# A batched matrix product in fp16: the wait for the last stores moves from SyncE to VectorE

## The chip, the cores and the metric

The kernel runs on one core of one Trainium2 chip. A core has TensorE (PE), VectorE (DVE), ScalarE (ACT), GpSimd (POOL) and SyncE (SP), each with its own instruction stream, and 16 DMA engines. The time is device microseconds of one execution; the median over three runs counts.

## The reference

```python
def setup_inputs():
    batch, dim_i, dim_j, dim_k = 32, 256, 512, 384
    return {
        "x": np.random.randn(batch, dim_i, dim_j).astype(np.float32),
        "y": np.random.randn(batch, dim_j, dim_k).astype(np.float32),
    }

def reference(x, y):
    return np.einsum('bij,bjk->bik', x, y).astype(np.float32)
```

For each of 32 batches a 256 x 512 matrix is multiplied by a 512 x 384 matrix. The inputs are 41.94 MB of float32, the output is 12.58 MB.

## The kernel before

The work is cut into N = 8 groups of Q = 4 batches. For each group SP loads x (2 MB) and y (3 MB), each in one DMA, into one of two buffers of each kind. POOL rounds x to fp16 (`round_x`) and y to fp16 (`round_y`). VectorE transposes x in 32 x 32 blocks (`transpose_x`), as 32-bit words that hold two fp16 numbers. TensorE multiplies: the four batches of a group lie in the four 32-row strips of the array, and a group is done in NE = 2 halves, each of which fills four PSUM banks. ScalarE and VectorE together copy the finished banks from PSUM into the output buffer `o_sb`, which holds the whole output; VectorE has the last five of sixteen blocks of each half (`OWN = 5`).

The order of the work is written out by hand: each engine has its own program with semaphores between them, most of them counted up through the whole kernel. At the head of the kernel stand the first four loads and a barrier of all engines (seen in the profile at lines 265 and 78). There is no barrier of the kernel's own at its end.

SP's program comes next. It loads groups 2 to 7 as buffers come free (lines 69 and 73, which wait on `s_cast`), and then issues three stores (line 96): groups 0 to 4 in one, groups 5 and 6 in one, and group 7. Each adds 16 to the semaphore `s_out` when it is complete. The last store waits for the last copies of ScalarE and VectorE (`s_act`, `s_dve`). Then, at line 110, SP gives a signal (`s_sp`) on which POOL clears all semaphores but `s_out`; and at line 111 SP waits until `s_out` has the 48 of the three stores and takes them off again, so that the next execution starts from zero. This wait is SP's last instruction.

VectorE's program ends in these lines, the last of which copies its share of the last half and signals `s_dve`:

```python
    vector_half(N - 1, 0)
    v.wait_ge(s_pe, chunk_done(N - 1, 1, NC - 1))
    collect(v.tensor_copy, N - 1, 1, BLOCKS[-OWN:], None, s_dve)
```

The copies of both engines are made by the helper `collect`, at line 165, and TensorE's products by `product`, at line 217.

## Time and profile before

| what | value |
|---|---|
| median of three runs | 132.0 us (131.89 to 132.18) |
| the profiled execution's own time | 132.13 us |
| its span, from the first to the last of the kernel's own instructions | 130.8 us |
| busy: PE, DVE, ACT, POOL | 61.4, 82.7, 84.1, 74.2 us |
| moved by DMA: read, written | 41.94 MB, 12.58 MB |
| mean over the span | 417 GB/s |

The profile is one execution. Its times are microseconds from the start of the span unless marked ns. The page gives for each engine a row of 40 digits, the busy tenths of 40 equal slices; further views list the timeline, the waits, the DMA issues, the busy time by windows, and all instructions of a source line. Instructions that only wait or signal (EVENT_SEMAPHORE, DRAIN) are not counted as busy; an engine's own queue of them is marked with a q, as in SPq. A wait is told as "who <- what released it: total us, times, longest".

### The profile page before, as it was taken

Reading aid. Unit: us, or ns where it says so; the run is one execution under the profiler, and the core shown is the slowest. Engines: PE = TensorE matmul, PEld = TensorE weight load, DVE = VectorE, ACT = ScalarE, POOL = GpSimd, SP = SyncE. Lnnn points to the kernel's source line nnn. Section 1 sums busy time; section 2 is a strip of 40 time slices with the busy share of each in tenths; the row PEclk is TensorE's granted clock in tenths of the full one; section 3 lists DMA queues with packets and bytes.
Section 4 is the critical chain, followed back from the end, with each engine's and each line's share of the span. In section 5 each row is a group of like instructions: output and inputs, shape, how many; then the busy total and the mean of one; then the engine's idle time right before and its main releaser. Section 6 shows DMA issues by size and latency. Waiting matters only on the chain. (4 is left out here: it accounts for less than half of the span.)

```text
span 130.8 us, 3199 instructions
## 1 busy us (share of the span) xinstructions
PE 61.4 (47%) x1024; PEld 46.7 (36%) x1024; DVE 82.7 (63%) x144; ACT 84.1 (64%) x178; POOL 74.2 (57%) x42
## 2 busy tenths in 40 slices
PE   0000009910992589089329905980975499100000
PEld 0000009800991566046129604970953236000000
DVE  0000036899379999985997997599999957920000
ACT  0400000599659989993998899399999957994000
POOL 0006991199929965992899459758973970000000
PEclk9999999995589689977986985599599959965555
DMA  5999999999999999999999999999999999999995
GB/s 120 451 396 441 421 431 451 443 408 428 451 413 421 438 443 401 436 436 443 423 458 398 443 408 466 398 418 436 463 398 408 427 438 425 436 428 421 425 440 248
DMA packets 3379, 54.55 MB, mean 417 GB/s; under 512 B 304, under 2 KB 304, under 8 KB 304
## 3 DMA queue, kind: packets, MB, share of 16 engines
q1 hardware_dynamic: 3376, 54.53, 98.1%
q14 instruction: 3, 0.02, 0.0%
HBM read 41.94 MB, written 12.58 MB: 417 GB/s over the span
## 5 line engine op out<-in xcount | busy, mean ns | idle before, releaser
L165 ACT COPY o_sb<-o_ps (+1 forms) x176 | 82.6, 469 | 31.7 <-PE o_ps L217 29.6
L217 PE MATMUL o_ps<-y_r,xt_sb 32*128 32x384 f16 x1024 | 61.4, 384 | 50.4 <-PEq L214 49.5
L217 PEld LDWEIGHTS o_ps<-y_r,xt_sb 32*128 32x128 f16 x1024 | 46.7, 107 | 64.6 <-issue 56.8
L156 DVE STREAM_TRANSPOSE xt_sb<-x_r 128x256 f32<-128x256 f32 x64 | 38.1, 626 | 30.9 <-POOL x_r L126 18.4
L136 POOL CAST y_r<-y_sb 128x1536 f16<-128x1536 f32 (+1 forms) x22 | 44.3, 2049 | 15.8 <-DMA y_sb<-in_y_dram 15.3
L165 DVE COPY o_sb<-o_ps 32x384 f32 (+1 forms) x80 | 44.6, 557 | 1.6
L126 POOL CAST x_r<-x_sb 128x2048 f16<-128x2048 f32 x16 | 30.2, 1893 | 16.8 <-DVE o_sb L165 12.1
L202 ACT ACT_TABLE_LOAD x1 | 1.3, 1283 | 3.4 <-PEq L78 3.4
L265 POOL MEMSET const-float32-0.0<- 128x1 f32 x1 | 0.1, 98 | 0.2 <-issue 0.2
L202 ACT COPY spare<-const-float32-0.0 1x1 f32<-1x1 f32 x1 | 0.2, 190 | 0.0
L265 POOL MEMSET const-bfloat16-1.0<- 128x1 bf16 x1 | 0.1, 101 | 0.0
L265 POOL MEMSET const-uint8-127<- 128x1 uint8 x1 | 0.1, 101 | 0.0
L265 POOL MEMSET const-float32-1.0<- 128x1 f32 x1 | 0.1, 98 | 0.0
## 6 DMA issues: line engine op xcount, KB each, us to landing
y_sb<-in_y_dram SPq DMA_DIRECT2D x8, 3072.0 KB, 16.8
x_sb<-in_x_dram SPq DMA_DIRECT2D x8, 2048.0 KB, 17.0
out_dram<-o_sb SPq DMA_DIRECT2D x1, 7680.0 KB, 33.9
out_dram<-o_sb SPq DMA_DIRECT2D x1, 3072.0 KB, 17.3
out_dram<-o_sb SPq DMA_DIRECT2D x1, 1536.0 KB, 11.5
```

The costliest lines, as they stand in the source:

```text
L126: po.tensor_copy(x_r[:, e], x_sb[n % 2][:, e * H : (e + 1) * H]).then_inc(s_cast, 1)
L136: ins = po.tensor_copy(y_r[:, s], y_sb[n % 2][:, s])
L156: v.transpose(xt_w[:, w], words[:, e, w]).then_inc(s_xt, 1)
L165: ins = copy(o_sb[g * PQ : (g + 1) * PQ, n, e, h], o_ps[h * PQ : (h + 1) * PQ, e * Q + g, :K],)
L202: a_.copy(spare, nc.const_aps.tensor(0.0, [1, 1], F32))
L217: return te.add_instruction(mybir.InstMatmult(name=nc.get_next_instruction_name(), start_tensor_calc=start, stop_tensor_calc=stop, tile_si ...
L265: nc = _bacc.Bacc("TRN2", target_bir_lowering=False, num_devices=1)
```

## The change

The wait for the 48 completions of the stores, with the subtraction that sets `s_out` back, is taken from the end of SP's program and stands at the end of VectorE's. It has the same condition and the same effect. In the changed kernel SP's last instruction is the signal to POOL at line 110, and the wait is at line 191; all lines of the kernel between the two places are one lower than before.

```diff
@@ -108,7 +108,6 @@
     sp.wait_ge(s_dve, NE)
     store(N - 1, N)
     sp.sem_inc(s_sp, 1)
-    sp.wait_op(s_out, 16 * 3, "sem-ge").then_inc(s_out, -16 * 3)
 
 
 
@@ -189,6 +188,7 @@
     vector_half(N - 1, 0)
     v.wait_ge(s_pe, chunk_done(N - 1, 1, NC - 1))
     collect(v.tensor_copy, N - 1, 1, BLOCKS[-OWN:], None, s_dve)
+    v.wait_op(s_out, 16 * 3, "sem-ge").then_inc(s_out, -16 * 3)
 
     a_ = nc.scalar
 
```

## The prediction

> **What bounds the kernel now.** I read the page first, for its head, the DMA rows and the chain.

> ```profile
> span 130.8 us, 3199 instructions
> ...
> DMA  5999999999999999999999999999999999999995
> GB/s 120 451 396 441 421 431 451 443 408 428 451 413 421 438 443 401 436 436 443 423 458 398 443 408 466 398 418 436 463 398 408 427 438 425 436 428 421 425 440 248
> ...
> q1 hardware_dynamic: 3376, 54.53, 98.1%
> ...
> ACT 8%; PE 2%; issue 0%
> ```

> All slices of the DMA row but the first and the last stand at 9: one queue keeps the 16 DMA engines busy for 98.1% of the span, at some 430 GB/s. The kernel is bound by its transfers from end to end. The chain of the page must be read with care here: it has 8% ACT and 2% PE because it follows instructions, and stops at the last copy that an instruction made; what runs after that is a store.

> Next the last stretch, in a view by windows (microseconds; busy time and count for PE, weight loads, DVE, ACT, POOL; then granted clock, DMA share, GB/s):

> ```profile
> core 0: us, PE busy (x) PEld busy (x) DVE busy (x) ACT busy (x) POOL busy (x), PEclk, DMA share, GB/s
> 109.80:119.30 9.50, 1.94 (x46) 1.19 (x37) 5.21 (x10) 9.21 (x20) 0.00 (x0) 0.78 1.00 427
> 119.30:130.30 11.00, 0.00 (x0) 0.00 (x0) 0.00 (x0) 0.00 (x0) 0.00 (x0) 0.50 0.93 398
> 130.30:130.80 0.50, 0.00 (x0) 0.00 (x0) 0.00 (x0) 0.00 (x0) 0.00 (x0) 0.50 0.00 0
> ```

> From 119.3 no engine computes, and the DMA engines work on alone to about 130.3. In the last half microsecond nothing moves any more: the completions of the last store are on their way. The changed instruction waits for just these. The timeline, the DMA issues and the waits of SP's queue give its place:

> ```profile
> 109.44 5.73 DVE L165 COPY o_sb<-o_ps 32x384 f32<-32x384 f32 x10
> ...
> 118.78 0.47 ACT L165 COPY o_sb<-o_ps 32x384 f32<-32x384 f32 x1
> 119.27 0.34 SPq L96 DMA_DIRECT2D out_dram<-o_sb  x1
> ```

> ```profile
> out_dram<-o_sb SPq DMA_DIRECT2D x1, 1536.0 KB, 11.5
> ```

> ```profile
> SPq L96 <- PE o_ps L217: 24.9, 2, 23.5
> SPq L111 <- SPq L111: 11.1, 1, 11.1
> SPq L108 <- DVE o_sb L165: 5.0, 1, 5.0
> SPq L96 <- ACT o_sb L165: 4.0, 1, 4.0
> ```

> The last store is issued at 119.27 and lands 11.5 us later: 119.27 + 11.5 = 130.77. SP's wait at L111, the longest of the tail with 11.1 us, ends there, and with it the span of 130.8. The profiled execution took 132.13 us, so 132.13 - 130.8 = 1.33 us lie around the span, before the first or behind the last of the kernel's own instructions; the trace does not divide them. The profiled time stands 0.1% above the median of 132.0.

> **The change, part by part.** Three things happen.

> SP loses one instruction. Its row, and the rows that show what the same kind of instruction costs on SP and on DVE (duration in ns: least, median, most; then first and last start in us), from the barriers at the head of the kernel:

> ```profile
> L111 SPq EVENT_SEMAPHORE  x1: 17/17/17, 130.8 to 130.8; - x1
> ```

> ```profile
> L78 POOLq EVENT_SEMAPHORE  x4: 17/17/17, 2.9 to 3.3; - x4
> L78 SPq DRAIN  x3: 7/7/123, 2.7 to 3.1; - x3
> ...
> L78 DVEq DRAIN  x2: 10/10/10, 0.8 to 3.2; - x2
> ...
> L78 SPq EVENT_SEMAPHORE  x2: 17/17/17, 3.0 to 3.4; - x2
> ...
> L78 DVEq EVENT_SEMAPHORE  x2: 21/21/21, 3.0 to 3.4; - x2
> ```

> The instruction takes 17 ns on SP and an instruction of its kind 21 ns on DVE. Both are released by the same landing at 130.77. So the end of the span moves by 21 - 17 = +4 ns. In both barrier rounds of L78 the two engines' waits start together at the tenth of a microsecond that the row shows (3.0 and 3.4), so a later wake-up of DVE is under 0.1 us; the term for the span is +0.00 to +0.10 us, and I take +0.00, since the rows are equal at that resolution.

> DVE gets that instruction behind its last copy. Is anything queued behind it? Nothing: it is the last of DVE's program, and DVE's ten last copies end at 109.44 + 5.73 = 115.17. The signal that SP needs from DVE for the last store is given by the last of these copies, ahead of the new wait. The wait that it starts at 115.17 lasts till 130.77, 15.6 us, and delays nobody. Cost zero; the cover is not needed, as no engine waits for DVE after that copy. No queue or DMA moves: the three stores are issued by the same instructions, at the same places, on SP. POOL's clearing of semaphores hangs on the signal that SP gives behind the last store, ahead of L111, and so stands as it is.

> What is left is the 1.33 us around the span. SP now reaches the end of its program at 119.27 + 0.34 = 119.61, plus 17 ns for the signal to POOL, some 11 us before the end, and DVE is the engine that is last. Whatever an engine does between its last instruction and the end of the execution was done by SP behind the landing; now SP does its share under the store, and DVE does its own behind the landing. The trace of before shows no row of that. Bounds: if all 1.33 us were SP's own work, and hid, the gain would be 1.33 us; if all of it were work of the engine that is last, and ran on DVE in the ratio of the rows above, the loss would be between 1.33 x (21/17 - 1) = 0.31 us and 1.33 x (10/7 - 1) = 0.57 us. The nearest row to such work is a barrier round of L78: SP's two waits start at 3.0 and 3.4, so a round of all engines costs some 0.4 us, of which SP and DVE have a drain and a wait each, 7 + 17 = 24 ns against 10 + 21 = 31 ns. A round with DVE last instead of SP thus differs by 7 ns. By that row I take 0.00 us for the exchange.

> [...] Row: 17 ns on SP, 21 ns on DVE, a ratio of 1.24. [...]

> Sum against the profiled execution: 132.13 + 0.00 (SP's instruction against DVE's) + 0.00 (DVE's queue) + 0.00 (what is around the span) = 132.13 us; against the median 132.0 us. I forecast 132.0 us. A difference of under 0.2%, 0.26 us, is about what a measurement of this kernel can tell from none.

> **The rivals.**

> Slower: DVE is the slower one to finish. Mechanism: behind the landing come further instructions of the runtime on the engine that is last, and each takes 21/17 to 10/7 of SP's time. For it speaks the ratio in two kinds of instruction; against it, that only a part of the 1.33 us can lie on that engine, as the rest is ahead of the first instruction or on others. Price at its full size +0.31 to +0.57 us, the middle +0.4 us: 132.4 us. It decides from the point at which about 0.86 us of the 1.33 are such work (0.26 / 0.31 x 1.33 = 1.1 us by the smaller ratio, 0.26 / 0.57 x 1.33 = 0.61 us by the larger, mean 0.86).

> Faster: SP has work of its own at its end, for which the others wait, and it now lies under the last store. For it speaks that SP is the engine that issued every transfer, and that its longest drain in L78, with transfers just issued, took 123 ns where DVE's took 10 ns; and there are 11 us of cover. Against it: two of SP's three drains there took 7 ns, less than DVE's. Price: one round like those of L78, 0.4 us, gone from the path: 131.6 us. It would need 0.26 us, two drains of 123 ns, to be seen. The extreme, with all 1.33 us gone, is 130.7 us, and no row makes it likely.

> That the change does not do what it says can hardly be: the wait needs all 48 counts of the three stores, wherever it stands. A variant is that DVE's wait ends late, because DVE has been idle for 15.6 us. The nearest rows are the waits of L78, after a pause of some 2 us: under 0.1 us later than SP. That stays within the forecast.

> **How the numbers follow.** The forecast, no difference beyond 0.2%, gets 0.42: every term that a row carries is of nanoseconds, but the part that would decide is the one that the trace does not show. Faster, 131.6 us: 0.30. Slower, 132.4 us: 0.28; the bound on it is firmer, since two ratios support it, but it needs most of the 1.33 us. The likeliest case alone covers 132.0 +- 0.26 us, 131.74 to 132.26. With the rivals' prices and 0.1 us of scatter about each (the three runs before lie between 131.89 and 132.18) the range is 131.5 to 132.5 us; what it leaves out is a gain that goes far beyond one round, or the larger ratio on all 1.33 us: under 2 in 10.

> **What would show it.** In the trace after, the DMA row and the issues are as before, the last store lands about 11.5 us after an issue at about 119.3, SP's last instruction is the signal at about 119.7, and the waits of SP's queue no longer have the entry of 11.1 us. DVE's last instruction is a wait of 21 ns which ends the span at about 130.8. The difference between the execution's own time and its span tells between the three cases: near 1.3 us, the forecast; near 0.9, the faster rival; near 1.7, the slower one. I would be wrong in the mechanism if the span itself changed by more than 0.3 us with the last landing where it was, or if the stores were issued at another time.

## The result, and the profile after

| | before | after |
|---|---|---|
| median | 132.04 us (131.82 to 132.43, 22 runs) | 132.22 us (132.00 to 132.98, 22 runs) |
| the profiled execution's own time | 132.13 us | 132.25 us |
| its span | 130.8 us | 130.8 us |

The ratio is 1.0017, 95% interval 1.0009 to 1.0024: the changed kernel is slower by 0.22 us (0.12 to 0.32). That is under the 0.2% that the prediction called no difference, and inside its range, but with 22 runs it is clear of zero.

The page of the changed kernel, in the lines that answer to those of before:

```profile
span 130.8 us, 3199 instructions
...
DMA  5999999999999999999999999999999999999996
...
q1 hardware_dynamic: 3376, 54.53, 98.3%
...
ACT 8%; PE 4%; issue 0%
```

Its last stretch by windows, with the same columns as before:

```profile
109.80:119.30 9.50, 2.34 (x57) 1.30 (x48) 5.20 (x10) 9.21 (x20) 0.00 (x0) 0.76 1.01 429
119.30:130.30 11.00, 0.00 (x0) 0.00 (x0) 0.00 (x0) 0.00 (x0) 0.00 (x0) 0.50 0.94 400
130.30:130.80 0.50, 0.00 (x0) 0.00 (x0) 0.00 (x0) 0.00 (x0) 0.00 (x0) 0.50 0.00 0
```

And the timeline's last store, its DMA issue, the waits of SP's queue, and the instructions of line 191, where the wait now stands:

```profile
119.27 0.34 SPq L96 DMA_DIRECT2D out_dram<-o_sb  x1
```

```profile
out_dram<-o_sb SPq DMA_DIRECT2D x1, 1536.0 KB, 11.5
```

```profile
SPq L96 <- PE o_ps L217: 25.2, 2, 23.6
SPq L108 <- DVE o_sb L164: 4.6, 1, 4.6
SPq L96 <- ACT o_sb L164: 4.1, 1, 4.1
```

```profile
L191 DVEq EVENT_SEMAPHORE  x1: 21/21/21, 130.8 to 130.8; - x1
```

Nothing else inside the span has changed: the last store is issued at 119.27 and takes 11.5 us, as before; the entry of 11.1 us is gone from SP's queue; a wait of 21 ns on DVE ends the span. In the trace's records the last completion comes at 130.722 and DVE's wait ends at 130.771, 49 ns later; before it was 130.767 and 130.801 on SP, 34 ns. The later start, 28 ns behind the completion instead of 17, is 27 or 28 ns in all four kernels of this document in which VectorE waits for the stores. So 0.015 us of the loss lie in the span. The rest of it lies outside: 132.25 - 130.771 = 1.479 us where it was 132.13 - 130.801 = 1.329 us.

This difference, an execution's own time less its span, is called **the rest** from here on. It is a far sharper measure than the time. The time moves by some tenths of a microsecond from run to run, and the span with it (130.5 to 131.5 us in the 22 runs of the changed kernel); the rest does not. Its mean over these runs is 1.480 us, with a scatter of 0.025 us, no more than the rounding of the listed spans to 0.1 us brings. For the kernel before it is 1.339 us over the 29 runs beside the first experiments, and 1.338 us over the 25 beside the later ones. So the rest grew by 0.141 us, and 0.141 + 0.015 = 0.156 us is the loss that the traces account for, against 0.18 us between the medians and 0.12 to 0.32 us by the ratio's interval.

### The profile page after: what moved, and what is told of

It is laid out like the page before. It is cut to its first block, busy times and chain, and to the rows that moved or that the text cites. A ratio compares the mean times of both kernels' runs of the same rounds, so it can differ in the third digit from the quotient of the medians.

```text
span 130.8 us, 3199 instructions
## 1 busy us (share of the span) xinstructions
PE 62.6 (48%) x1024; PEld 45.2 (35%) x1024; DVE 82.7 (63%) x144; ACT 84.1 (64%) x178; POOL 74.2 (57%) x42
## 3 DMA queue, kind: packets, MB, share of 16 engines
q1 hardware_dynamic: 3376, 54.53, 98.3%
## 5 line engine op out<-in xcount | busy, mean ns | idle before, releaser
L217 PE MATMUL o_ps<-y_r,xt_sb 32*128 32x384 f16 x1024 | 62.6, 388 | 49.5 <-PEq L214 49.5
L217 PEld LDWEIGHTS o_ps<-y_r,xt_sb 32*128 32x128 f16 x1024 | 45.2, 108 | 66.6 <-issue 56.4
## 6 DMA issues: line engine op xcount, KB each, us to landing
out_dram<-o_sb SPq DMA_DIRECT2D x1, 1536.0 KB, 11.5
```

What stands on the lines that cost most here:

```text
L217: return te.add_instruction(mybir.InstMatmult(name=nc.get_next_instruction_name(), start_tensor_calc=start, stop_tensor_calc=stop, tile_si ...
```

## The experiments

Three theories of the 0.14 us stood at first. By the clock theory, what follows the last instruction runs on the engine that is last, in proportion to its instruction times. By the chain theory, the engines meet one after the other, and the place of the engine that arrives last decides, and nothing else (the last-arriver theory of a later expectation). By the third, each engine has a stretch of its own behind its last instruction, and the execution is over when the last of these is.

**The same wait on the three other engines.** In each, the line is taken from SP and put at the end of another engine's program.

```diff
-    sp.wait_op(s_out, 16 * 3, "sem-ge").then_inc(s_out, -16 * 3)
...
# one of these, as the last instruction of its engine
+    a_.wait_op(s_out, 48, "sem-ge").then_inc(s_out, -48)
+    po.wait_op(s_out, 48, "sem-ge").then_inc(s_out, -48)
+    te.wait_op(s_out, 48, "sem-ge").then_inc(s_out, -48)
```

> ScalarE waits for the 48 completions as its last instruction, instead of SyncE. The measure is the execution's own time less its span (the rest): 1.33 us with SyncE as the last engine, 1.48 us with VectorE. Clock theory: what follows the last instruction runs on the last engine, in proportion to its instruction times; a wait takes 17 ns on ScalarE as on SyncE, so the rest is 1.33 us and the time that of the kernel before (132.0 us). Chain theory: the engines meet at the end one after the other, and the place of the last engine in that order decides; ScalarE then has a rest of its own, other than 1.33 by more than 0.03 us, with the sign given by its place.

> GpSimd waits for the 48 completions, behind its clearing of the semaphores. Clock theory: 17 ns for a wait as on SyncE, rest 1.33 us, time 132.0 us. Chain theory: a rest of its own, between that with ScalarE and that with VectorE if the order of the engines is a simple row of them.

> TensorE waits for the 48 completions. Clock theory by instruction times: a wait takes 51 ns there against 17 on SyncE; VectorE's 21 against 17 made 0.15 us, so the work on the last engine is 0.15 / (21/17 - 1) = 0.64 us on SyncE and 1.9 us on TensorE: the rest grows by 1.28 us to 2.6 us and the time to 133.3 us. Chain theory: the rest differs from 1.33 us by some tenths at most, so 1.1 to 1.6 us, and the time lies between 131.8 and 132.3 us.

The last instructions of the three, by their lines, ScalarE first, then GpSimd, then TensorE:

```profile
L209 ACTq EVENT_SEMAPHORE  x1: 17/17/17, 130.8 to 130.8; - x1
```

```profile
L145 POOLq EVENT_SEMAPHORE  x1: 17/17/17, 130.7 to 130.7; - x1
```

```profile
L250 PEldq EVENT_SEMAPHORE  x1: 51/51/51, 131.5 to 131.5; - x1
```

| engine that waits | its wait, ns | mean rest, us (runs) | above SP | ratio of times to before (95%) |
|---|---|---|---|---|
| SyncE (before) | 17 | 1.339 (29) | - | - |
| VectorE (the change) | 21 | 1.480 (22) | 0.141 | 1.0017 (1.0009 to 1.0024) |
| ScalarE | 17 | 1.506 (10) | 0.167 | 1.0013 (1.0001 to 1.0024) |
| TensorE | 51 | 1.616 (8) | 0.277 | 1.0037 (1.0019 to 1.0054) |
| GpSimd | 17 | 1.889 (10) | 0.550 | 1.0037 (1.0024 to 1.0049) |

The clock theory falls. ScalarE's and GpSimd's waits take the same 17 ns as SP's, yet their rests are 0.17 and 0.55 us longer; TensorE's wait is three times as long, and its rest is 1.62 us, not 2.6. That ScalarE has a rest of its own is what the chain theory expected; TensorE's lies just above the 1.1 to 1.6 us that it gave. SP is the best of the five. GpSimd's rest does not lie between ScalarE's and VectorE's either, as a simple row of engines would have it. The times follow the rests less sharply: ScalarE's and VectorE's can't be told apart by them, and TensorE's span was longer in the profiled execution, 131.5 us, because the last completion came late, at 131.445 (two more of its eight runs have spans of 131.3 and 131.4 us).

**A relay: VectorE ends just ahead of SyncE.**

```diff
-    sp.wait_op(s_out, 16 * 3, "sem-ge").then_inc(s_out, -16 * 3)
+    sp.wait_op(s_out, 49, "sem-ge").then_inc(s_out, -49)
...
     collect(v.tensor_copy, N - 1, 1, BLOCKS[-OWN:], None, s_dve)
+    v.wait_op(s_out, 48, "sem-ge").then_inc(s_out, 1)
```

> VectorE waits for the 48 completions and adds one; SyncE waits for 49 and takes them off, so that SyncE is last and VectorE ends just ahead of it. The span grows by the hand-over, some 0.05 us. If VectorE's own work behind its last instruction is what is longer (clock theory), it still ends last: the time is that of the changed kernel, 132.2 us, and the rest, counted from SyncE's end, 1.43 us. If the engine that arrives last alone decides (chain theory), the rest goes back to 1.33 us and the time is 132.1 us.

The two last instructions, DVE's and SP's:

```profile
L192 DVEq EVENT_SEMAPHORE  x1: 21/21/21, 131.3 to 131.3; - x1
```

```profile
L111 SPq EVENT_SEMAPHORE  x1: 17/17/17, 131.4 to 131.4; - x1
```

In the records DVE's wait ends at 131.355 and SP's at 131.397, 0.042 us later. The mean rest, counted from SP's end, is 1.436 us (10 runs). Counted from DVE's end it is 1.436 + 0.042 = 1.478 us: VectorE's 1.480 again, though SP was the last to arrive. The chain theory falls in that form, the last arriver alone; a chain in which each engine also has some work of its own is not excluded by it. The time is 132.23 us, ratio 1.0020 (1.0007 to 1.0032), as the theory of own stretches has it.

**The same relay from GpSimd**, whose stretch is the longest:

```diff
-    sp.wait_op(s_out, 16 * 3, "sem-ge").then_inc(s_out, -16 * 3)
+    sp.wait_op(s_out, 49, "sem-ge").then_inc(s_out, -49)
...
+    po.wait_op(s_out, 48, "sem-ge").then_inc(s_out, 1)
```

> As the relay with VectorE, but GpSimd waits for the 48 completions and adds one, and SyncE waits for 49 and is last. Own-tail theory (each engine has a stretch of its own behind its last instruction, and the execution ends when the last of these ends): GpSimd's is 1.89 us against SyncE's 1.34, so the rest, counted from SyncE's end some 0.05 us later, is 1.84 us, and the time 132.5 us. Last-arriver theory (only the identity of the engine that ends last decides): rest 1.34 us, time 132.1 us.

The mean rest is 1.855 us (10 runs). GpSimd's wait ends at 130.486 in the records, SP's at 130.528, 0.042 us later; 1.889 - 0.042 = 1.847 us was due. The time is 132.54 us, ratio 1.0037 (1.0024 to 1.0050).

**The relay with a gap.** VectorE hands over as in the first relay, but SP has some more to do, so that VectorE ends well ahead of it.

```diff
+    s_pad = nc.alloc_semaphore("s_pad")
...
-    sp.wait_op(s_out, 16 * 3, "sem-ge").then_inc(s_out, -16 * 3)
+    sp.wait_op(s_out, 49, "sem-ge").then_inc(s_out, -49)
+    for _ in range(4):
+        sp.sem_inc(s_pad, 1)
+    sp.wait_op(s_pad, 4, "sem-ge").then_inc(s_pad, -4)
...
+    v.wait_op(s_out, 48, "sem-ge").then_inc(s_out, 1)
```

> The relay with VectorE, and SyncE then has four more signals and a wait of its own, so that VectorE ends some 0.2 to 0.3 us ahead of SyncE. Own-tail theory: VectorE's stretch is 0.14 us longer than SyncE's and is now over before SyncE's is, so the rest falls to 1.34 us, whereas it was 1.44 us in the relay without the gap. Theory that a late VectorE costs in any case: the rest stays at 1.44 us or above. The time is that of the relay plus the gap in either case, less 0.1 us by the first theory.

DVE's wait, SP's four signals and SP's last wait:

```profile
L196 DVEq EVENT_SEMAPHORE  x1: 21/21/21, 130.6 to 130.6; - x1
```

```profile
L114 SPq EVENT_SEMAPHORE  x4: 17/17/17, 130.7 to 130.8; - x4
```

```profile
L115 SPq EVENT_SEMAPHORE  x1: 17/17/17, 130.9 to 130.9; - x1
```

DVE ends at 130.585 and SP at 130.933, a lead of 0.35 us (0.2 to 0.3 us had been expected), more than the 0.14 by which DVE's stretch is longer. The mean rest is 1.345 us (10 runs), that of SP as the only late engine. So a late VectorE costs only as far as its own stretch reaches beyond that of SP. The time, 132.37 us, ratio 1.0031 (1.0017 to 1.0046), is longer by the gap itself, as it had to be.

**Does the length come from VectorE's program or its pause?** The changed kernel, with 64 signals more on VectorE between its last copy and the wait.

```diff
+    s_pad = nc.alloc_semaphore("s_pad")
...
     collect(v.tensor_copy, N - 1, 1, BLOCKS[-OWN:], None, s_dve)
+    for _ in range(64):
+        v.sem_inc(s_pad, 1)
+    v.wait_op(s_pad, 64, "sem-ge").then_inc(s_pad, -64)
     v.wait_op(s_out, 16 * 3, "sem-ge").then_inc(s_out, -16 * 3)
```

> VectorE waits as in the changed kernel, but 64 signals and a wait on them stand between its last copy and the wait for the stores, done while the last store is under way. If the longer end belongs to the engine, the rest stays at 1.48 us. If it came from the length or place of the program (what is fetched behind the last instruction), or from the long pause ahead of the wait, it moves by more than 0.03 us.

```profile
L193 DVEq EVENT_SEMAPHORE  x64: 21/21/21, 112.4 to 118.2; - x64
```

The signals run until 118.2, and the mean rest is 1.480 us (10 runs), the very value without them. Neither 64 more instructions in front of it, nor a pause that starts some 3 us later, moves it. The time is 132.37 us, ratio 1.0027 (1.0015 to 1.0038); its interval overlaps that of the change, and what its median has beyond 132.22 lies in the spans (mean 130.89 against 130.76 us), not in the rest.

**What lies behind the last instruction.** No view of the profile has a row there, but the records of the same traces list the updates of all semaphores with their times, and these go on behind the span. Semaphore 2, which none of the kernel's instructions touches, is updated nine times just ahead of the span, over 0.371 us in the trace of before, and nine times at the end. In the trace of before four of these last nine come while the last store is still under way: 0.175 us after TensorE's last instruction, 0.114 us after ScalarE's, 0.537 us after GpSimd's, and one 0.044 us after that, when VectorE had long ended. The other five come behind SP's wait. With another engine last, more of the nine are left (times in us, each from the one profiled execution of its kernel):

| last engine | updates behind its end | own part: from its end to the first | way: from the first to the last | together: its stretch | the rest of this execution |
|---|---|---|---|---|---|
| SyncE (before) | 5 | 0.136 | 0.164 | 0.300 | 1.329 |
| VectorE (the change) | 6 | 0.195 | 0.250 | 0.445 | 1.479 |
| GpSimd | 7 | 0.566 | 0.284 | 0.850 | 1.914 |
| ScalarE | 8 | 0.149 | 0.322 | 0.471 | 1.502 |
| TensorE | 9 | 0.234 | 0.359 | 0.593 | 1.615 |

The records don't name the engine that makes an update, but the counts and times let it be read: in these executions the engines met in a chain, TensorE, ScalarE, GpSimd, VectorE, SyncE, in the trace of before at 111.912, 119.360, 120.402, 120.446 and 130.937, and four more updates followed SyncE's, from 130.981 to 131.101. Which engines make these four was not shown. Each of the five gave its update when the one ahead of it had done so and it was through with what it did itself behind its last instruction. A last engine's stretch thus has two parts, which the table calls its own part and its way. In the kernel in which ScalarE waits, only one update comes before ScalarE's end, TensorE's, though GpSimd, VectorE and SyncE had ended more than 11 us before.

The stretches account for the differences: those of VectorE, ScalarE, TensorE and GpSimd are 0.145, 0.171, 0.293 and 0.550 us longer than SyncE's, and their mean rests 0.141, 0.167, 0.277 and 0.550 us. The relays agree: the last of the nine comes 0.445 us after VectorE's end in the first, as in the changed kernel; 0.853 us after GpSimd's end in the second; and 0.294 us after SP's end in the relay with the gap. So the chain theory and the theory of own stretches are each right in half: each engine has an own part, and its place in the chain decided how many steps followed, from four behind SyncE's update to eight behind TensorE's. Of VectorE's 0.145 us, 0.059 are the longer own part and 0.086 the longer way. Nearly all of ScalarE's loss and most of TensorE's are the way (0.158 of 0.171 and 0.195 of 0.293 us); most of GpSimd's, 0.430 of 0.550 us, is the own part.

**What stays open.** What an engine does in its own part is not in the records, and so neither is why GpSimd's is four times that of SyncE. What follows the chain is the same for all, or nearly: updates of almost all other semaphores, and 0.79 to 0.83 us after the chain's end a second round of nine on semaphore 2. The rest less the stretch is 1.02 to 1.04 us in seven of the nine profiled executions, and 1.06 and 1.07 us in the two in which that second round began latest behind the chain. How much of this lies ahead of the first instruction was not told apart; it drops out of the differences.

## Why the prediction was right or wrong

**The span: right.** The stores, their landing, SP's signal and POOL's clearing are where they were. The term for wait and wake-up was taken as +0.00 out of 0.00 to 0.10 us; it measured +0.015 us, of which 4 ns are 21 against 17 ns, and 11 ns the later start behind the last completion (28 against 17 ns).

**DVE's queue: right.** Nothing stood behind the wait, and 64 instructions ahead of it changed nothing in the rest.

**The exchange at the end: wrong.** The step that failed is "By that row I take 0.00 us for the exchange". It took a barrier round at the head of the kernel as the nearest row, in which SP and DVE differ by 7 ns. The ends of the two engines differ by 0.141 us, twenty times that: an own part of 0.195 us on VectorE against 0.136 on SyncE, and a way through the chain of 0.250 us in five steps against 0.164 us in four. The term lay within the bounds that stood there, from a gain of 1.33 to a loss of 0.57 us, but the value was read from a row that shows only how long a drain and a wait took with an engine ready, 24 ns on SyncE against 31 on VectorE, and nothing of an engine's end or of its place. The prediction also took it that the trace shows nothing of that end. No row of a view does, but the semaphore updates in the trace of before have the whole chain, with VectorE's place ahead of SyncE's, and so a longer way if VectorE is last. There is a difference of 0.22 us (0.12 to 0.32), then, where none was forecast; it is so small that the measured time still lies within the 0.26 us that the prediction took for none, and within its range.

**The slower rival: right in its direction, right in half of its mechanism, wrong in its price.** It had VectorE as the slower one to finish, at 0.31 to 0.57 us; the price is 0.14 us. It scaled the 1.33 us by the ratio of instruction times. VectorE's own part is 0.195 / 0.136 = 1.4 times SyncE's, near its larger ratio, but only 0.136 us of the 1.33 are such work, and the longer way through the chain, more than half of the loss, it did not have. Nor do instruction times order the own parts of all engines: ScalarE's and GpSimd's are 0.149 and 0.566 us with SP's 17 ns for a wait, TensorE's 0.234 us with 51 ns. VectorE's wait is the longer one, 21 against 17 ns, but the ends of ScalarE, TensorE and GpSimd, 0.17, 0.28 and 0.55 us longer than SP's, are not in the order of their waits of 17, 51 and 17 ns.

The longer way is in the records. In the trace of before the steps behind SyncE's update take 44, 39, 34 and 47 ns; in that of the changed kernel those behind VectorE's take 24, 106, 40, 34 and 46 ns. VectorE's way is 0.086 us longer than SyncE's, ScalarE's 0.158 and TensorE's 0.195. The own parts, 0.136 to 0.566 us, come on top.

**The faster rival: wrong in its sign.** SP does have an own part, 0.136 us, and in the changed kernel it no longer stands ahead of SP's update, which follows VectorE's by 24 ns. But VectorE's own part and its longer way stand in its place, and SP has the shortest end of the five, 0.300 us against 0.445 to 0.850. No run ties its drain of 123 ns, with transfers just issued, to that end, 11 us after its last issue.

**The test that the prediction named** was the right one. It asked for the difference between own time and span, and would have read 1.3, 0.9 or 1.7 us; 1.48 us is between the forecast and the slower rival, and it was the measure that decided every experiment.

## What to carry to other kernels

Behind this kernel the engines met in a chain, and the engine that was last cost what it did itself behind its last instruction, 0.136 us on SyncE to 0.566 us on GpSimd, and all the steps that followed its place, 0.164 us behind SyncE's update to 0.359 us behind TensorE's. SyncE's end was the shortest, with VectorE 0.14, ScalarE 0.17, TensorE 0.28 and GpSimd 0.55 us behind, so the last wait of this kernel belongs on SyncE, and another engine that finishes late has to be ahead of it by as much as its end is longer: VectorE 0.35 us ahead left the rest at SyncE's, 1.345 us. To measure a change at the very end, compare own time less span instead of the times: it showed 0.14 us at once, where the times needed 22 runs. And where no view has a row, look at the records of semaphore updates: they told what the views left open.

## What the runs showed of the hardware that was not expected

VectorE's signals did not wait for its copies. In the kernel with 64 signals behind the last copy, the first runs at 112.4, as shown above, while the ten last copies go on to 109.46 + 5.73 = 115.19 in its timeline:

```profile
109.46 5.73 DVE L165 COPY o_sb<-o_ps 32x384 f32<-32x384 f32 x10
```

The signals come every (118.216 - 112.362) / 63 = 93 ns by the records; the first and the last of SyncE's four signals in the relay with a gap start at 130.670 and 130.849, one every 60 ns.
